# Two-layer attention stack and gated block on one core: the weighted sums for the gates and for layer 1's shift and scale, on GpSimd instead of VectorE

## The chip, the cores and the metric

The kernel runs on one NeuronCore of a Trainium2 chip. Its five engines have instruction queues of their own, each issued strictly in order: TensorE (PE in the profile; its weight loads are shown apart as PEld), VectorE (DVE), ScalarE (ACT), GpSimd (POOL) and SyncE (SP), which issues all of this kernel's DMAs. The metric is device time in microseconds, from one execution; lower is better. What can be told from no change in a measurement of this kernel is about 2%.

## The reference, cut to what matters

256 tokens of 1024 features pass through two layers with adaptive normalization, a final norm, and a second block (three gated branches and a feed-forward network). Everything is float32. What the change touches is `ada`, a product of one vector of 1024 features with a matrix:

```
c_act = jax.nn.silu(c)
for layer in range(DEPTH):
    ada = jnp.einsum('bd,de->be', c_act, w_ada[layer]) + b_ada[layer]
    shift, scale, gate = jnp.split(ada, 3, axis=-1)
    h = rms_norm(x, norm_g[layer]) * (1.0 + scale[:, None, :]) + shift[:, None, :]
    i = layer // 2
    if layer % 2 == 0:
        y = even_mixer(h, ...)
    else:
        y = odd_mixer(h, ...)
    x = x + gate[:, None, :] * y
return rms_norm(x, final_g)
```

## The kernel before, in words

Tokens lie in two tiles of 128, features in eight tiles of 128. A projection is a sum over feature tiles of matrix products of 128x128 by 128x512. For accuracy each float32 operand is split into a rounded part and the rest (`split`, line 616): ScalarE copies the rounded part into a tile of the pool `kr`, VectorE subtracts to get the rest into another, and TensorE makes three products of them (`mm3`). Weights come by DMA in pieces of 512 KB, 128x1024, into the pool `k4`, which has 13 slots and also holds other tiles of that size; a slot is free again once its piece has been split. So per piece VectorE and ScalarE work once, and TensorE 12 times.

The stages in the order of time: the norm of layer 0 and its first products (up to about 60 us); the rest of layer 0's projections with its attention between them, and the first half of its output projection (up to about 210 us); its second half, with the residual sum and the norm of layer 1 (`end0`, line 1372, and `next_tile`, line 1390); layer 1 (up to about 480 us); the second block.

`ada` is computed in two ways. Layer 0's shift and scale have code of their own (`ada_v`, `ada_p`), which the change leaves alone. For layer 0's gate and for all three parts of layer 1 there is `ada_row` (line 1284), called for eight chunks of 512 columns: two for `gate0`, two for the shift `B1`, two for the scale `A1`, two for layer 1's gate `gate1`. A chunk has eight feature tiles; the weights of two of them come in one DMA of 512 KB. `st["acc"]`, 128x512 from the pool `k2` (14 slots), is cleared by GpSimd, gets the bias in its first row by DMA, and is then added to eight times: weights times a column of `sc`, plus the sum so far, in one VectorE instruction. That makes 64 such instructions. Then `last` splits the sum (ScalarE, VectorE), TensorE multiplies both parts by ones (`onesr`), which adds up the 128 partitions and spreads the result over all of them, and the row is evicted from the PSUM bank `m`.

The order of the instructions is not written by hand. The program is run once as a draft, in which `Order` (line 127) collects every instruction with what it reads and writes; a list schedule with a price for each kind of instruction (`cost`, line 474) then sets the order on every engine and which slot each tile gets, and the program is issued in that order (`issue`, line 439). All instructions pass through one call, so the profile names line 527 for nearly all of them, and tiles are told by pool: `k` is `k4` or `k2`, `kr` the split parts, `acc` and `m` PSUM banks. Once the order is set, an engine that waits for an operand holds up all that is behind it in its queue; that holds for SP as well, where a load that waits for a slot holds up the loads behind it.

Of the kernel before, what the change touches and what calls it, by code (L numbers as in the profile page):

```python
# [21 lines left out]
P = 128  # L22
# [6 lines left out]
# columns of w_in_even, in the order in which the kernel uses them  # L29
# [9 lines left out]
def plan():  # L39
    """(name, where it comes from, k-tiles, columns, queue) of every weight chunk, in the order of use."""  # L40
# [65 lines left out]
# rows that are broadcast over the partitions  # L106
_ROWS = [("bg0", 1024), ("b1", 3072), ("g1", 1024), ("fg", 1024), ("mg", 1024), ("ffg", 1024),
         ("gb", 3072), ("sink", 8)]
# per-partition columns
# [17 lines left out]
class Order:  # L127
    """Collects the instructions of the kernel, with what each reads and writes, and issues them in the
    order of a list schedule: first by program order, then by the latest start that each instruction
    can have without lengthening the schedule found before. A tile takes any slot of its pool that is  # L130
    free by then, so long as every tile that still holds one can finish."""

    def __init__(self, nc, found):
        self.ops = []                  # [engine, call, duration, row share, tiles, predecessors, table, name, lag]
        self.hist = {}                 # tile -> [(region, op, writes)]
        self.tiles = {}                # tile -> its pool
        self.found, self.count = found, 0
        self.vector, self.scalar = Engine(self, "DVE", nc.vector), Engine(self, "ACT", nc.scalar)
        self.tensor, self.gpsimd = Engine(self, "PE", nc.tensor), Engine(self, "Pool", nc.gpsimd)
        self.sync = Engine(self, "SP", nc.sync)  # L140
        self.lag = 0.0

    def tile(self, pool, shape, dt):
        """a tile of the pool: a place of its own in the draft, a slot that is free by then in the issue"""
# [15 lines left out]
    def region(ap):  # L160
        """(partitions, elements) that an access covers, as bounds"""
# [44 lines left out]
    def gap(self, i, j):  # L206
        """from the end of op i to the start of op j that needs it"""
        a, b = self.ops[i], self.ops[j]
        return DELAY.get((a[0], b[0]), 230.0)
# [7 lines left out]
    def late(self, end):  # L217
        """the ops put as late as the engines allow, those first that ended last; the time from their start to the end"""
# [24 lines left out]
    def best(self, slack, rounds):  # L243
        self.links()
        # first the order of the program; then, from the order found, the ops as late as they may be
# [8 lines left out]
    def solve(self, slack, way):  # L254
# [5 lines left out]
        # tiles: the op that takes the slot, and the ops that hold it  # L260
# [20 lines left out]
        held = {}                                        # ops that wait for a slot, by pool  # L281
# [3 lines left out]
        def wants(i):  # L285
            """the tiles of op i that have no slot yet"""
            return [t for t in ops[i][4] if t not in slot]

        def safe(p, new):
            """whether the program's own order could still go on once `new` are taken as well"""  # L290
# [26 lines left out]
        def room(i):  # L317
            """when the slots that op i needs are there, or None"""
# [30 lines left out]
        while done < n:  # L349
# [36 lines left out]
            else:  # L386
                if e == "PE":
                    # the clock is halved after a tick with little to do
# [62 lines left out]
# from the end of an instruction to the start of one that needs it, by their engines  # L451
# [11 lines left out]
def columns(name, writes, reads):  # L463
    """what the clock's monitor counts of a matrix instruction: columns, by the share of the rows"""
# [9 lines left out]
def cost(engine, name, writes, reads, kw):  # L474
# [32 lines left out]
    if engine == "ACT":  # L507
        return (51.0 if psum else 93.0) + 0.833 * r + 93.0 * pointers, 230.0, SETS.get(kw.get("func"))
    return 80.0 + 0.75 * r, 230.0, None
# [22 lines left out]
def body(tc: tile.TileContext, *args, dbg=None):  # L532
    """The program runs twice: once to find the order of its instructions and the slots of its tiles,
    with nothing issued, and once to issue them."""
# [8 lines left out]
def program(ctx: ExitStack, tc: tile.TileContext, found, x_d, wst, rows, cols, rope, w2, out, dbg=None):  # L543
# [65 lines left out]
    def weight(key, part=0):  # L609
        """the two parts of a piece of the weights, loaded and split where it is first needed"""  # L610
# [17 lines left out]
    # ---------------- the tensor engine's order: products of the projections, and between every few  # L628
    # of them what else is due ----------------
# [29 lines left out]
    class Proj:  # L659
        """One chunk of 512 columns; lhs = (hi, lo), of four feature tiles [P, 4, 256] each; evict(tt, psum) per token tile."""  # L660
# [33 lines left out]
    def out_proj(tag, lhs, evict, mid):  # L694
        """two chunks; first the first half of the contraction, then the second, one token tile after the other"""
# [26 lines left out]
    # additive masks: token on the partition, key along the row  # L722
# [5 lines left out]
    # strictly causal, for both token tiles side by side, and a column past the end of each: there the scores are  # L728
    # large, so that a running product starts anew
# [10 lines left out]
    # compressed blocks: a token sees block n once it is at 16 n + 31 or past it  # L740
# [15 lines left out]
    def rsqrt(ssum, scale, n=1, post=None):  # L756
        """1 / sqrt(ssum * scale + EPS) of a [P, n] tile: a first guess from the bits, then Newton."""
# [7 lines left out]
        # r <- (v r r - 3 m) r leaves -2, 16 and -8192 times the root  # L765
# [19 lines left out]
    def to_lhs(lhs, src, tt, k0=0, nk=8, scale=None):  # L785
        """src [P tokens, nk*128] -> feature-major hi and lo."""
# [15 lines left out]
    def rope_to(outs, src, tt, n):  # L802
        """src [P, n*64] (PSUM) -> every AP of outs [P, n, 64]."""
# [10 lines left out]
    def silu_of(dst, z):  # L814
        """2 silu(z) = z (1 + tanh(z / 2)); z in PSUM."""
# [13 lines left out]
    def transposes(dst, src, n, p):  # L829
        """dst [P, n, 128] (SBUF) <- n transposed 128-column blocks of src, by way of the bank p."""  # L830
# [5 lines left out]
    # the heads of a unit lie on the same half of the partitions: products of different halves  # L836
    # run side by side and may not share a bank
# [3 lines left out]
    def sm_unit(tt, segs, klen, masks, o, den, sink=None):  # L841
        """segs: (pairs lhsT and rhs, values per key block, slot); masks: (view, rhs) adders on the scores.
        Three steps, each of which returns the next."""
# [59 lines left out]
    # =====================================================================================  # L903
    # layer 0
    # =====================================================================================
# [67 lines left out]
    kd = [t4([P, 5, 2, 64], n="kd") for _ in range(2)]        # ka, ks0, ks1, kw0, kw1, each twice  # L973
    kcr = t4([P, 2, 2, 2, 64], n="kcr")                        # [tt, (k, v), group, d]
    va = const.tile([P, 2, 64], F32, name="va")
    vsw = t4([P, 2, 2, 2, 64], n="vsw")                        # [tt, (slc, win), group, d]
    gb = const.tile([P, 2, 24], F32, name="gb")
    qaT = t2([P, 4, P], n="qaT")                               # the first token tile
    qaS, qbS = (t4([P, 2, 4, P], F32R) for _ in range(2))      # the second, in two parts (see `stack`)
    qbT = t4([P, 4, 256], n="qbT")  # L980
    kT = t2([P, P], n="kaT")
    kaS = t4([P, 2, 256], F32R)                                # [part, token]
# [881 lines left out]
```

## Time and profile before

| what | us |
|---|---|
| runs of the kernel | 807.18, 811.31, 822.17 (median 811.31) |
| span of the profiled execution | 810.1 |
| TensorE busy | 786.1 |
| VectorE busy | 601.2 |
| ScalarE busy | 393.8 |
| GpSimd busy | 8.8 |

The span is the time from the first to the last instruction of one profiled execution. Busy is the time in which at least one instruction of the engine runs; since products are pipelined, TensorE shows as busy when it is merely full of overlapping work. The granted clock (PEclk) is the share of 2.4 GHz that TensorE was given; it has two levels, 1.00 and 0.50 (1.2 GHz), and a stretch shows the mean. A line of a group has the mean duration of one instruction in ns; an idle time with a releaser is what the engine waited for just before.

### The profile page before, as it was taken

What the parts mean: (1) busy time and instruction counts of PE and PEld (TensorE: products, weight loads), DVE (VectorE), ACT (ScalarE), POOL (GpSimd) and SP (SyncE); (2) the same over time, 40 slices, a digit from 0 to 9 for tenths busy, and PEclk for the clock granted to TensorE, in tenths of its full rate; (3) what the DMA queues carried; (4) which work ended last, traced back from release to release, by engine and by line L of the source; (5) the groups of instructions that cost most, each with busy time, mean ns of one, the idle gap of its engine ahead of it and who ended that gap; (6) DMA issues with size and microseconds to landing.
All of it is one profiled execution on the core that took longest, in us unless ns stands there. A gap on an engine that the chain in (4) does not pass through costs nothing.

```text
span 810.1 us, 10521 instructions
## 1 busy us (share of the span) xinstructions
PE 786.1 (97%) x3716; PEld 617.3 (76%) x3716; DVE 601.2 (74%) x1129; ACT 393.8 (49%) x683; POOL 8.8 (1%) x34
## 2 busy tenths in 40 slices
PE   4999999999799999999999999999999999999998
PEld 3886567778677777777887777888887888888886
DVE  7989877868998644657879999999887555556541
ACT  4363556544355644554665545456465543445410
POOL 2000000000000000000000000000000000000000
PEclk9999999978899999999999999999999999999999
DMA  9995677445386325272753446654484645646301
GB/s 334 336 329 175 207 261 235 152 185 177 108 324 241 113 81 182 75 234 77 264 189 108 136 137 218 210 197 133 161 292 150 227 155 177 201 143 221 116 1 52
DMA packets 43443, 148.11 MB, mean 183 GB/s; under 512 B 5880, under 2 KB 7288, under 8 KB 43392
## 3 DMA queue, kind: packets, MB, share of 16 engines
q1 hardware_dynamic: 43392, 147.46, 53.6%
q8 instruction: 29, 0.48, 0.2%
q14 instruction: 22, 0.18, 0.1%
HBM read 146.39 MB, written 1.05 MB: 182 GB/s over the span
## 4 chain that ended last, share of the span: by engine, by line
PE 90%; DMA 3%; DVE 3%; ACT 2%; issue 1%; ACTq 0%; SPq 0%
PE acc L527 71%; PE m L527 19%; DMA k<-in_wst_dram 3%; DVE k L527 2%; ACT kr L527 1%; ACT k L527 1%; DVE kr L527 1%; DMA x<-in_x_dram 0%; DVE tiny L527 0%; DVE ab L527 0%; DVE sc L527 0%; DVE b L527 0%; DVE qkn L527 0%; ACTq L527 0%; SPq L527 0%
## 5 line engine op out<-in xcount | busy, mean ns | idle before, releaser
L527 PE MATMUL acc<-kr,kr 128*128 128x512 f32 x2520 | 662.3, 409 | 3.8 <-ACT kr L527 3.4
L527 PEld LDWEIGHTS acc<-kr,kr 128*128 128x128 f32 x2520 | 469.9, 190 | 111.9 <-ACT kr L527 5.8
L527 DVE TENSOR_TENSOR kr<-k,kr 128x1024 fp32r<-128x1024 f32 (+3 forms) x238 | 269.2, 1144 | 81.3 <-PE acc L527 65.9
L527 ACT ACTIVATE kr<-k 128x1024 fp32r<-128x1024 f32 (+3 forms) x238 | 234.3, 998 | 190.1 <-PE acc L527 126.3
L527 PE MATMUL m<-identf,k 128*128 128x128 f32 (+1 forms) x434 | 103.0, 283 | 13.3 <-DVE sc L527 8.7
L527 PEld LDWEIGHTS m<-k,k 128*128 128x128 f32 (+1 forms) x404 | 67.6, 197 | 23.2 <-issue 13.3
L527 ACT ACTIVATE k<-m 128x512 f32<-128x512 f32 (+5 forms) x96 | 45.3, 489 | 78.1 <-PE m L527 73.3
L527 PE MATMUL m<-k,k 128*128 128x64 f32 (+3 forms) x404 | 82.7, 302 | 0.4 <-DVE k L527 0.4
L527 PEld LDWEIGHTS m<-identf,k 128*128 128x128 f32 (+1 forms) x434 | 60.7, 149 | 26.5 <-issue 16.9
L527 DVE SCALAR_TENSOR_TENSOR k<-k,sc,k 128x512 f32<-128x512 f32 (+1 forms) x112 | 69.1, 629 | 0.3
L527 DVE SCALAR_TENSOR_TENSOR k<-k,col,k 128x256 f32<-128x256 f32 x128 | 54.3, 476 | 0.0
L527 DVE TENSOR_REDUCE tiny<-m 128x2 f32<-128x512 f32 (+1 forms) x30 | 20.7, 692 | 43.1 <-PE m L527 42.3
L527 ACT ACTIVATE kr<-m 128x512 fp32r<-128x512 f32 (+3 forms) x56 | 27.3, 498 | 39.2 <-PE m L527 34.9
L527 ACT ACTIVATE k<-m,tiny 128x128 f32<-128x128 f32 (+1 forms) x80 | 32.8, 421 | 26.9 <-DVE tiny L527 12.7
L527 DVE TENSOR_TENSOR kr<-m,kr 128x512 fp32r<-128x512 f32 (+3 forms) x52 | 28.3, 557 | 8.5 <-ACT kr L527 6.1
L527 PE MATMUL m<-kr,kr 128*128 128x408 f32 (+2 forms) x96 | 29.9, 377 | 0.0
L527 DVE TENSOR_TENSOR k<-k,k 128x512 f32<-128x512 f32 (+4 forms) x41 | 25.0, 615 | 1.1 <-PE m L527 0.9
L527 PEld LDWEIGHTS m<-kr,kr 128*128 128x128 f32 (+1 forms) x96 | 18.8, 201 | 7.3 <-issue 4.1
L527 DVE SCALAR_TENSOR_TENSOR k<-acc,rf,k 128x256 f32<-128x256 f32 x22 | 10.4, 481 | 13.3 <-ACT k L527 13.1
L527 DVE SCALAR_TENSOR_TENSOR k<-k,acc 128x512 f32<-128x512 f32 x20 | 13.6, 682 | 7.5 <-PE acc L527 4.5
L527 ACT ACTIVATE k<-acc,rf 128x256 f32<-128x256 f32 x22 | 10.2, 472 | 17.3 <-PE acc L527 17.0
L527 DVE TENSOR_TENSOR k<-acc,x 128x512 f32<-128x512 f32 x4 | 2.8, 692 | 20.4 <-PE acc L527 20.4
(100 smaller groups left out, 337.3 us busy)
## 6 DMA issues: line engine op xcount, KB each, us to landing
k<-in_wst_dram SPq DMA_DIRECT2D x266, 512.0 KB, 4.3
k<-in_rows_dram SPq DMA_DIRECT2D x4, 512.0 KB, 4.0
k<-in_wst_dram SPq DMA_DIRECT2D x8, 204.0 KB, 4.4
k<-in_rows_dram SPq DMA_DIRECT2D x6, 256.0 KB, 5.2
x<-in_x_dram SPq DMA_DIRECT2D x2, 512.0 KB
out_dram<-k SPq DMA_DIRECT2D x4, 256.0 KB, 2.0
k<-in_w_dram SPq DMA_DIRECT2D x2, 128.0 KB
rp<-in_rope_dram SPq DMA_DIRECT2D x1, 128.0 KB, 6.5
```

The lines of the kernel that those rows point to most:

```text
L527: self._o.add(self._n, lambda: f(*a, **kw), method, writes, reads, info)
```

## The change

In `ada_row` the one VectorE instruction becomes two on GpSimd: the weights are multiplied in place by the column of `sc`, and the product is added to the sum. The price list of the schedule gets an entry for a GpSimd addition. Comments are taken out elsewhere.

```diff
@@ cost
     if engine == "ACT":
         return (51.0 if psum else 93.0) + 0.833 * r + 93.0 * pointers, 230.0, SETS.get(kw.get("func"))
+    if name == "tensor_tensor":
+        return 100.0 + 2.2 * r, 230.0, None
     return 80.0 + 0.75 * r, 230.0, None
@@ ada_row, part
-                V.scalar_tensor_tensor(st["acc"], st["raw"][:, r % 2, :], sc[:, r:r + 1], st["acc"], op0=ALU.mult, op1=ALU.add)
+                w = st["raw"][:, r % 2, :]
+                G.tensor_scalar(w, w, sc[:, r:r + 1], None, op0=ALU.mult)
+                G.tensor_tensor(st["acc"], w, st["acc"], op=ALU.add)
                 if r == 7:
                     after(3, last)
```

The schedule is made anew, so the order of all engines and the slots differ. In the rows below, a name with two numbers is a tile: `k46_67` is slot 6 of `k4`, `k20_107` slot 0 of `k2`, `sc_179` the column of weights.

First VectorE and GpSimd where the first chunk of `gate0` is summed, just after layer 0's first products. Before, on VectorE:

```order
L527 SCALAR_TENSOR_TENSOR k20_107<-k46_67,sc_179,k20_107 128x512
L527 TENSOR_TENSOR k47_68<-k211_118,k29_116 128x128
L527 SCALAR_TENSOR_TENSOR k20_107<-k46_67,sc_179,k20_107 128x512
L527 TENSOR_TENSOR k211_118<-k210_117,k212_119 128x512
L527 TENSOR_TENSOR k47_68<-k25_112,k26_113 128x128
L527 TENSOR_TENSOR k210_117<-acc3_150,rp_172 128x512
L527 SCALAR_TENSOR_TENSOR k20_107<-k40_61,sc_179,k20_107 128x512
L527 TENSOR_TENSOR k212_119<-k28_115,k210_117 128x512
L527 TENSOR_TENSOR kr18_95<-m3_157,kr18_95 128x128
L527 SCALAR_TENSOR_TENSOR k20_107<-k40_61,sc_179,k20_107 128x512
L527 TENSOR_TENSOR kr18_95<-m2_156,kr18_95 128x128
```

Now on GpSimd, from its last early clear to the end of that chunk:

```order
L529 MEMSET k45_66 128x2x2
L529 TENSOR_SCALAR k412_73<-k412_73,sc_179 128x512 x2
L529 TENSOR_TENSOR k20_107<-k412_73,k20_107 128x512 x2
L529 TENSOR_SCALAR k46_67<-k46_67,sc_179 128x512 x2
L529 TENSOR_TENSOR k20_107<-k46_67,k20_107 128x512
L529 TENSOR_SCALAR k411_72<-k411_72,sc_179 128x512
L529 TENSOR_TENSOR k20_107<-k46_67,k20_107 128x512
L529 TENSOR_SCALAR k411_72<-k411_72,sc_179 128x512
L529 TENSOR_TENSOR k20_107<-k411_72,k20_107 128x512
L529 TENSOR_SCALAR k412_73<-k412_73,sc_179 128x512
L529 TENSOR_TENSOR k20_107<-k411_72,k20_107 128x512
L529 TENSOR_SCALAR k412_73<-k412_73,sc_179 128x512
```

The additions into `k20_107` are gone from VectorE and stand on GpSimd, each with a multiplication ahead of it.

Next TensorE at the border of layer 0 and layer 1, where the first half of the output projection ends (`acc3_150`), the finished rows are added up (`onesr`), and the transposes for the second half come (`identf`). Before:

```order
L527 MATMUL acc3_150<-kr11_88,kr1_78 128x512
L527 MATMUL m3_157<-kr16_93,onesr_174 128x512 x2
L527 MATMUL m1_155<-kr22_99,onesr_174 128x512
L527 MATMUL m2_156<-kr19_96,onesr_174 128x512
L527 MATMUL m1_155<-kr22_99,onesr_174 128x512
L527 MATMUL m2_156<-kr19_96,onesr_174 128x512
L527 MATMUL m0_154<-kr23_100,onesr_174 128x512 x2
L527 MATMUL m2_156<-identf_160,k412_73 128x128 x4
L527 MATMUL acc0_147<-kr18_95,kr15_92 128x512
L527 MATMUL acc0_147<-kr20_97,kr15_92 128x512
```

Now:

```order
L529 MATMUL acc3_150<-kr18_95,kr3_80 128x512
L529 MATMUL m0_154<-kr13_90,onesr_174 128x512 x2
L529 MATMUL m1_155<-kr25_102,onesr_174 128x512
L529 MATMUL m3_157<-kr16_93,onesr_174 128x512
L529 MATMUL m1_155<-kr25_102,onesr_174 128x512
L529 MATMUL m3_157<-kr16_93,onesr_174 128x512
L529 MATMUL m2_156<-kr15_92,onesr_174 128x512 x2
L529 MATMUL m1_155<-kr12_89,onesr_174 128x512
L529 MATMUL m2_156<-identf_160,k49_70 128x128 x4
```

Four rows were taken there, both parts of each; now it is these four and the first part of a fifth, `kr12_89`, the first chunk of `gate1`, whose second part stands about a hundred rows further down.

Last SP's queue, with what each load waits for, at about the second and third chunk. Before:

```order
L527 DMA k46_67<-in_wst_dram 128x1024 [waits DMAHW6_49,DVE_49]
L527 DMA k40_61<-in_wst_dram 128x1024 [waits DMAHW7_49,DVE_49]
L527 DMA k410_71<-in_wst_dram 128x1024 [waits DMAHW1_49,DVE_49]
L527 DMA k212_119<-in_rows_dram 1x512 [waits DMAHW0_49,Pool_49]
L527 DMA k412_73<-in_wst_dram 128x1024 [waits DMAHW3_49,DVE_49]
L527 DMA k27_114<-in_rows_dram 1x512 [waits DMAHW2_49,Pool_49]
L527 DMA k411_72<-in_wst_dram 128x1024 [waits PE_49]
L527 DMA k43_64<-in_wst_dram 128x1024 [waits DMAHW4_49,PE_49]
L527 DMA k49_70<-in_wst_dram 128x1024 [waits DMAHW5_49,PE_49]
L527 DMA k410_71<-in_wst_dram 128x1024 [waits DMAHW7_49,DMAHW6_49,DVE_49]
L527 DMA k46_67<-in_wst_dram 128x1024 [waits PE_49]
```

Now:

```order
L529 DMA k412_73<-in_wst_dram 128x1024 [waits DMAHW3_49,DMAHW1_49,Pool_49]
L529 DMA k49_70<-in_wst_dram 128x1024 [waits DMAHW2_49,PE_49,Activation_49]
L529 DMA k46_67<-in_wst_dram 128x1024 [waits DMAHW5_49,Pool_49]
L529 DMA k47_68<-in_wst_dram 128x1024 [waits DMAHW4_49,DVE_49]
L529 DMA k40_61<-in_wst_dram 128x1024 [waits PE_49,Activation_49]
L529 DMA k43_64<-in_wst_dram 128x1024 [waits DMAHW6_49,DMAHW0_49,DVE_49]
L529 DMA k411_72<-in_wst_dram 128x1024 [waits DMAHW7_49,Pool_49]
L529 DMA k412_73<-in_wst_dram 128x1024 [waits DMAHW1_49,Pool_49]
L529 DMA k213_120<-in_rows_dram 1x512 [waits Pool_49]
L529 DMA k47_68<-in_wst_dram 128x1024 [waits DMAHW4_49,DMAHW2_49,Pool_49]
L529 DMA k43_64<-in_wst_dram 128x1024 [waits DMAHW6_49,DMAHW3_49,Pool_49]
```

Loads of weights (`in_wst_dram`) that waited for VectorE to give a slot back wait for GpSimd now, where the slot held a piece of `ada`; the loads behind them in the queue include those for the projections.

## Rows read from the trace of the kernel before

**Rows 1.** The page, busy us (share of the span) and instructions of each engine.

```profile
PE 786.1 (97%) x3716; PEld 617.3 (76%) x3716; DVE 601.2 (74%) x1129; ACT 393.8 (49%) x683; POOL 8.8 (1%) x34
```

**Rows 2.** Windows by stage: length, busy us of each engine, PEclk, DMA share, GB/s.

```profile
0.00:60.00 60.00, 45.97 (x221) 38.85 (x222) 51.18 (x136) 28.61 (x49) 5.58 (x27) 1.00 0.93 334
60.00:110.00 50.00, 49.31 (x240) 30.05 (x239) 43.82 (x106) 23.90 (x66) 1.57 (x3) 1.00 0.60 201
110.00:164.00 54.00, 54.00 (x292) 40.29 (x290) 43.37 (x81) 30.85 (x94) 1.68 (x4) 1.00 0.63 217
164.00:200.00 36.00, 36.00 (x174) 29.86 (x173) 25.56 (x61) 17.73 (x35) 0.00 (x0) 0.76 0.47 165
200.00:222.00 22.00, 17.32 (x71) 13.69 (x70) 20.94 (x49) 8.18 (x16) 0.00 (x0) 0.84 0.37 117
222.00:262.00 40.00, 39.92 (x186) 31.20 (x184) 36.91 (x46) 21.06 (x25) 0.00 (x0) 1.00 0.78 283
262.00:480.00 218.00, 218.00 (x1049) 167.73 (x1047) 156.26 (x313) 115.07 (x202) 0.00 (x0) 1.00 0.43 142
480.00:810.00 330.00, 325.57 (x1496) 265.65 (x1496) 223.13 (x345) 148.43 (x200) 0.00 (x0) 1.00 0.51 168
```

**Rows 3.** The page, the chain that ended last, share of the span by engine.

```profile
PE 90%; DMA 3%; DVE 3%; ACT 2%; issue 1%; ACTq 0%; SPq 0%
```

**Rows 4.** The chain in order of time at the layer border: start, us, what.

```profile
212.23 1.70 ACT k L527 x4
213.94 2.71 issue
...
222.97 5.79 DMA k<-in_wst_dram
```

**Rows 5.** Timeline of DVE, first sum and layer border: start, us, form.

```profile
64.05 0.74 DVE L527 SCALAR_TENSOR_TENSOR k<-k,sc,k 128x512 f32<-128x512 f32 x1
...
205.10 0.74 DVE L527 SCALAR_TENSOR_TENSOR k<-k,sc,k 128x512 f32<-128x512 f32 x1
...
207.89 0.74 DVE L527 SCALAR_TENSOR_TENSOR k<-k,sc,k 128x512 f32<-128x512 f32 x1
```

**Rows 6.** DVE from 60 to 262 us by form: busy us, mean ns, idle before.

```profile
L527 DVE SCALAR_TENSOR_TENSOR k<-k,sc,k 128x512 f32<-128x512 f32 x64 | 47.0, 742 | 0.0
L527 DVE TENSOR_TENSOR kr<-k,kr 128x1024 fp32r<-128x1024 f32 x38 | 45.7, 1214 | 0.3 <-ACT kr L527 0.3
...
L527 DVE TENSOR_TENSOR k<-k,k 128x512 f32<-128x512 f32 x12 | 8.2, 683 | 0.9 <-PE m L527 0.9
...
L527 DVE TENSOR_TENSOR kr<-k,kr 128x512 fp32r<-128x512 f32 x8 | 5.4, 681 | 0.5 <-ACT kr L527 0.5
...
L527 DVE SCALAR_TENSOR_TENSOR k<-k,tiny,k 128x512 f32<-128x512 f32 x4 | 2.9, 744 | 0.0
...
L527 DVE TENSOR_TENSOR k<-x,k 128x512 f32<-128x512 f32 x4 | 2.7, 682 | 0.0
L527 DVE TENSOR_TENSOR x<-x,k 128x512 f32<-128x512 f32 x4 | 2.7, 688 | 0.0
```

**Rows 7.** All of POOL by form.

```profile
L527 POOL MEMSET k<- 128x512 f32 x10 | 5.2, 525 | 109.1 <-PE m L527 85.7 <-ACT kr L527 13.9 <-DVE kr L527 9.5
...
L527 POOL TENSOR_SCALAR_AFFINE_SELECT mc<-mc 128x16 f32<-128x16 f32 x2 | 0.3, 198 | 0.0
...
masks.py:199 POOL TENSOR_SCALAR_AFFINE_SELECT identf<-identf 128x128 f32<-128x128 f32 x1 | 0.3, 292 | 0.1
```

**Rows 8.** Timeline of PE at the layer border.

```profile
210.63 2.03 PE L527 MATMUL m<-kr,onesr 128*128 128x512 f32 x8
216.65 0.66 PE L527 MATMUL m<-identf,k 128*128 128x128 f32 x2 [3.99 <-issue]
```

**Rows 9.** Waits of SP's queue from 60 to 262 us: total, times, longest.

```profile
SPq L527 <- DVE k L527: 51.1, 20, 15.7
...
SPq L527 <- POOL k L527: 6.3, 2, 5.2
```

## The prediction

> **What bounds the kernel now.** I read the busy table first, then windows by stage, then the chain, then the forms of the two engines between which the work moves. The reader is to see in the busy table that TensorE is at 97% of the span and GpSimd at 1% [rows 1], and in the chain that 90% of it is TensorE's own work and 3% VectorE's [rows 3]. A VectorE at 74% is therefore no bound by itself. The windows say where it might still be one [rows 2]. From 110 to 164 us TensorE is busy for all 54 us, from 262 to 480 us for all 218. Idle it is 14.0 us up to 60 us, 0.7 us from 60 to 110, 4.7 us from 200 to 222 and 4.4 us after 480. The 64 sums all lie between 60 and 262 us [rows 6], so of TensorE's idle time only 0.7 + 4.7 + 0.1 = 5.5 us is there to be won.
>
> A second loss is the clock. It is 0.76 from 164 to 200 us and 0.84 from 200 to 222 us, at full speed elsewhere in this part [rows 2], which means stretches at 1.2 GHz; (1 - 0.76) x 36 + (1 - 0.84) x 22 = 12.2 us is what they cost at most. Before the first fall VectorE is far from full, 25.56 of 36 us; TensorE is in the short products of the attention there, full by its records.
>
> **What is removed.** 64 instructions of 742 ns, 47.0 us of VectorE, with no idle time before them [rows 6]. Behind a full TensorE this is worth nothing; it counts where TensorE waits for VectorE. That place is the layer border. TensorE adds up the finished rows from 210.63 us and then stands still for 3.99 us ahead of the transposes of layer 1's input [rows 8]; in the chain this is the norm of layer 1, on ScalarE and VectorE [rows 4], and VectorE is busy for 20.94 of the 22 us [rows 2]. But only two of the sums stand ahead of that norm there, at 205.10 and 207.89 us [rows 5]. So the gain on the path is 2 x 0.74 = 1.5 us. The other 62 I cost at nothing; the cover is TensorE's own queue, and if that cover were not full, the 5.5 us above would be their limit. The stall behind the border that ends with a load of weights of 5.79 us [rows 4] depends on slots and not on VectorE's load, and I leave it as it is.
>
> **What is added.** 64 multiplications and 64 additions on GpSimd, 128x512 each. The trace has no GpSimd instruction that reads two tensors. A clear of that size, which only writes, takes 525 ns. An operation with one input takes 198 ns for 16 elements and 292 ns for 128 [rows 7], which is 0.84 ns an element on a fixed 185 ns, and makes 292 + 384 x 0.84 = 615 ns for 512. Lower end of a step of one multiplication and one addition: two clears, 1.05 us. Upper end: every tensor read or written is a pass of its own, two for the multiplication and three for the addition, 5 x 0.43 + 2 x 0.185 = 2.52 us. I take 0.62 us, and for the addition a second read behind the first, 0.62 + 0.43 = 1.05 us, together 1.66 us, because the one-input operation is the nearest row. 64 steps are then 106 us (67 to 161). The Trainium skill, page "GPSIMD Engine Reference", section "Elementwise — side-by-side cycle accounting", has 4497 ns for an addition of 2048 elements; an estimate from it is 1.1 us for 512 and 1.7 us a step, 109 us in all.
>
> GpSimd has the time. Its only other work from 60 to 262 us is 3.3 us of clears [rows 2]. The tightest stretch is from the first sum, 64.05 us [rows 5], to the row at the border, 210.63 us [rows 8]: by then TensorE's new order wants the first part of a fifth row there, beside two earlier ones, so seven chunks or 56 steps must be done in 146.6 us, 2.6 us each. At 1.66 us that is 93 us, cover for 53 us of waiting.
>
> Three queues now wait for GpSimd. ScalarE's copy of a finished sum waits, and behind it are the copies of weights; TensorE's product with ones waits, and behind it everything; and SP's loads wait for the slots of `ada` pieces, with the projections' weights behind them. SP waited for such slots before as well, 51.1 us for VectorE's work on `k` tiles in 20 waits, without TensorE running dry [rows 9]; with a slot held for two steps of 1.66 us instead of two of 0.74 it is held 1.8 us longer, and I cost that at 0 as long as GpSimd keeps its pace. Its clears for attention and for new sums stand behind sums in the same queue; they are few and early.
>
> **What may be paid twice.** While GpSimd reads, VectorE may have to wait, or the other way round. No row shows the two at work together on tensors, so the cost is bounded from both sides. Below: 0. Above: they exclude each other whenever a VectorE instruction takes two inputs from SBUF. The large ones of that kind between 60 and 262 us are 45.7 + 8.2 + 5.4 + 2.9 + 2.7 + 2.7 = 67.6 us in 70 instructions [rows 6]. GpSimd holds the inputs for 106 of 198 us, 54% of the time; what is left of an operation when another arrives is (0.62² + 1.05²) / (2 x 1.67) = 0.44 us on average, so a wait is 0.24 us. From 204 to 222 us I count 27 such instructions, large and small, in VectorE's timeline; if all wait, the border grows by 27 x 0.24 = 6.5 us. I take the middle, 3.2 us, as no row is nearer to either end. Elsewhere VectorE has won 47 us and pays back less than that, so TensorE stays covered.
>
> On this the Trainium skill has a rule against the change: "SBUF — State Buffer", section "Who interferes with whom", says that a VectorE instruction with two SBUF inputs and a GpSimd instruction that reads SBUF lock each other out for a whole instruction. No run here shows it yet; by that rule the upper end holds, and its result is the first rival.
>
> **The sum.** 810.1 us of the profiled span - 1.5 + 3.2 = 811.8. The median of the runs is 811.3, 1.2 us above the span, which I add: 813. Within the forecast's own range of 806 to 820 lie the 0 and the 6.5 us above, and some us from a new order that moves the clock's stretches. The products are the same ones in much the same sequence, so I expect a stretch at 1.2 GHz at the end of the attention again.
>
> **Rivals.**
> 1. Reads exclude each other throughout, GpSimd keeps its pace: 810.1 - 1.5 + 6.5 + 1.2 = 816. For it speaks how much of VectorE's work has two inputs; against it nothing that a row could show. Within 2% all the same.
> 2. Slower: GpSimd falls behind. It has 2.6 us for a step. With the upper end of 2.52 us and two waits for VectorE (67.6 of 202 us, a third of the time, half of about 1 us left: 0.17 us each) a step is 2.9, and with the slots that then come back late to SP some 3.0 us: 56 x 3.0 = 168 us instead of 146.6, TensorE stands 21.5 us longer at the border, 833 us. For it: queues in order, SP's loads behind GpSimd, a fifth row wanted at the border. Against it: it needs 1.8 times the price that the nearest rows give. It decides from 2.6 us on; at 3.2 us it would be 844.
> 3. Faster: the relief lets the norm and the attention end sooner, and both the 4.7 us of idle time and the 12.2 us of clock go: 810.1 - 16.9 + 1.2 = 794. For it: VectorE is 95% busy from 200 to 222 us. Against it: only three of the sums are in that window, and the clock falls while VectorE is not full.
>
> That the change does not do what it says is out: the order has 128 more tensor instructions on GpSimd, and 64 fewer on VectorE.
>
> **How the numbers follow.** About 2%, 16 us, is what a measurement of this kernel can tell from no change: faster is below 795, slower above 827.5. Forecast 0.47, rival 1 0.15, rival 2 0.30, rival 3 0.08. The first two are within 2% (0.62), the third gives slower (0.30), the fourth faster (0.08). The range reaches from near rival 3 to near the far end of rival 2: 797 to 842.
>
> **What would show it.** Right: VectorE's busy time falls by 40 to 47 us, GpSimd's rises by about 106, TensorE's busy time and its idle time at the border stay within some us, and the clock is low again in the last part of the attention. Exclusion would show as two-input instructions of VectorE with a mean well above 1214 ns and 683 ns while those with one SBUF input keep theirs. Rival 2 would show as waits of ScalarE, TensorE and SP for GpSimd, and a GpSimd without idle time up to the border. Wrong I am if TensorE's idle time between 60 and 262 us grows by more than 16 us, or nearly vanishes along with the low clock.

## The result, and the profile after

The changed kernel takes 864.0 us (median of 4 runs, 861.33 to 868.46) against 810.6 us for the kernel before on the same chip. The ratio is 1.067 with a 95% interval of 1.0615 to 1.0726: slower, by 53 us, and outside the range of 797 to 842. Some runs of these kernels are slow, at a lower clock; one of the four of before is (822.17 us, without which the difference is 54 us), and ratios and the medians of the experiments are of the other runs. The profiled execution spans 859.6 us, 49.5 more than before.

The busy times of the changed kernel, on the page, stand against [rows 1]:

```profile
PE 805.5 (94%) x3716; PEld 624.9 (73%) x3716; DVE 587.0 (68%) x1065; ACT 393.7 (46%) x683; POOL 208.3 (24%) x162
```

GpSimd has taken on 199.5 us and not 106. VectorE has given up 47.0 us and yet fell by only 14.2: by the sum of durations it is 33 us longer in the work that it kept (22.8 us against the 564.2 us of cols8 below, which has the same order and hardly any work on GpSimd). TensorE has the same 3716 instructions; its idle time (span less busy time) went from 24.0 to 54.1 us, and its busy time up by 19.4 us. The two make the 49.5 us. The chain that ended last now has GpSimd in it, where [rows 3] had 90% of TensorE:

```profile
PE 70%; POOL 15%; DVE 7%; issue 3%; DMA 3%; ACT 1%; POOLq 0%; SPq 0%; DVEq 0%; ACTq 0%
```

The windows by stage, cut as in [rows 2] (length; busy us of PE, PEld, DVE, ACT, POOL; PEclk, DMA share, GB/s):

```profile
60.00:110.00 50.00, 46.23 (x195) 27.70 (x194) 32.38 (x76) 18.30 (x51) 44.81 (x34) 0.90 0.44 157
110.00:164.00 54.00, 50.21 (x254) 33.42 (x253) 33.08 (x57) 27.45 (x83) 45.11 (x30) 1.00 0.53 187
164.00:200.00 36.00, 27.73 (x120) 20.43 (x120) 11.70 (x20) 11.03 (x27) 36.00 (x25) 0.78 0.31 105
200.00:222.00 22.00, 18.28 (x82) 13.95 (x82) 14.11 (x27) 12.04 (x26) 21.84 (x16) 0.73 0.72 240
222.00:262.00 40.00, 30.73 (x125) 24.44 (x124) 34.59 (x64) 16.59 (x28) 29.13 (x20) 0.80 0.45 158
262.00:480.00 218.00, 211.46 (x1001) 164.15 (x1000) 141.78 (x266) 107.91 (x187) 21.82 (x12) 0.98 0.45 157
```

From 164 to 200 us GpSimd is busy for the whole 36 us, and TensorE, VectorE and ScalarE all have idle time at once. TensorE is idle for 28.8 us from 60 to 262 us (5.5 before), and the clock is at 0.73 to 0.80 for nearly 100 us, after windows in which TensorE had gaps. That the gaps brought it down is not shown: in the kernel before it fell to 0.76 behind 54 us without one [rows 2]. One minus the clock, times the length, adds up to 26.9 us from 60 to 262 us, where [rows 2] gave 12.2: stretches at 1.2 GHz are at most 14.7 of the 19.4 us of longer busy time.

GpSimd's two new forms:

```profile
L529 POOL TENSOR_SCALAR k<-k,sc 128x512 f32<-128x512 f32 x64 | 113.9, 1787 | 76.1 <-DMA k<-in_wst_dram 76.1
L529 POOL TENSOR_TENSOR k<-k,k 128x512 f32<-128x512 f32 x64 | 88.0, 1379 | 1.0
```

A step is 1.79 + 1.38 = 3.17 us, against the 1.66 us of the forecast. The 76.1 us of idle time include 49.7 us before the first step; from then to the border, 190 us, GpSimd rests for 15.8 us, 13.8 of them from 105 us on, for a load. Its timeline shows one multiplication with nothing in its way:

```profile
198.65 1.56 POOL L529 TENSOR_SCALAR k<-k,sc 128x512 f32<-128x512 f32 x1
```

Who waits for it (total, times, longest), from 56 to 290 us; in [rows 9] SP's queue waited 6.3 us for GpSimd:

```profile
ACT kr L529 <- POOL k L529: 39.5, 6, 9.6
...
PEld m L529 <- ACT k L529: 20.9, 17, 8.2
...
PE m L529 <- ACT k L529: 15.2, 7, 7.8
```

```profile
SPq L529 <- POOL k L529: 153.9, 33, 12.0
```

TensorE itself hardly waits for GpSimd: it waits for ScalarE, which stands in its own queue behind a copy that waits for GpSimd. The chain in order of time has GpSimd in long pieces up to 219 us, and again behind the border, where its last eight steps stand:

```profile
63.10 17.05 POOL k L529 x11
...
144.87 29.02 POOL k L529 x20
...
183.85 17.66 POOL k L529 x12
...
202.64 10.16 POOL k L529 x7
212.86 6.34 POOL k L529 x4
...
264.10 5.03 POOL k L529 x3
...
270.49 7.09 POOL k L529 x3
277.66 7.14 POOL k L529 x4
```

And the finished rows on TensorE, at 210.63 us in [rows 8], with the transposes of layer 1's input behind them:

```profile
246.19 2.03 PE L529 MATMUL m<-kr,onesr 128*128 128x512 f32 x8
249.38 0.50 PE L529 MATMUL m<-kr,onesr 128*128 128x512 f32 x1 [1.17 <-ACT k L529]
256.32 1.08 PE L529 MATMUL m<-identf,k 128*128 128x128 f32 x4 [6.44 <-DVE k L529]
```

So 246.19 - 210.63 = 35.6 of the 49.5 us are lost before the rows, and 13.9 behind them. Up to the rows TensorE has 19.8 us more idle time and is busy 15.8 us longer, in 969 instructions (968 before), at a mean clock of 0.91 (0.96 before). The rows follow on its own products without a gap, and it waits only 1.17 us among them: the time was lost on the way there. The longer idle time behind the rows, 6.44 us, ends with VectorE. Its forms from 60 to 290 us, against [rows 6]:

```profile
L529 DVE TENSOR_TENSOR kr<-k,kr 128x1024 fp32r<-128x1024 f32 x34 | 49.4, 1459 | 17.5 <-ACT kr L529 17.2
L529 DVE TENSOR_TENSOR k<-acc,rp 128x512 f32<-128x512 f32 x14 | 9.0, 681 | 0.0
...
L529 DVE TENSOR_TENSOR kr<-m,kr 128x512 fp32r<-128x512 f32 x10 | 6.8, 685 | 3.1 <-ACT kr L529 3.1
...
L529 DVE SCALAR_TENSOR_TENSOR k<-k,tiny,k 128x512 f32<-128x512 f32 x4 | 3.8, 960 | 0.0
L529 DVE TENSOR_TENSOR x<-x,k 128x512 f32<-128x512 f32 x4 | 3.7, 958 | 0.0
...
L529 DVE TENSOR_SCALAR tiny<-tiny 128x4 f32<-128x4 f32 x6 | 1.8, 298 | 0.1
```

and three of these forms in the kernel before, from 55 to 310 us:

```profile
L527 DVE TENSOR_TENSOR k<-acc,rp 128x512 f32<-128x512 f32 x24 | 15.5, 683 | 0.3 <-PE acc L527 0.3
...
L527 DVE TENSOR_TENSOR kr<-m,kr 128x512 fp32r<-128x512 f32 x10 | 6.9, 687 | 0.9 <-ACT kr L527 0.8
...
L527 DVE TENSOR_SCALAR tiny<-tiny 128x4 f32<-128x4 f32 x8 | 1.3, 162 | 0.1
```

With both inputs in SBUF these means rose: 1214 to 1459 ns, 744 to 960, 688 to 958. Not every such form did: `k<-x,k` of 128x512 took 686 ns, 682 before. With one input in PSUM (`acc`, `m`) they are 681 and 685, against 683 and 687. But VectorE's small TENSOR_SCALAR instructions, with one tensor input in SBUF, rose too, the last line from 162 to 298 ns. The profile alone thus offers two causes, GpSimd's own slowness and a lock between the two engines, and besides them a new order of all instructions, made with wrong prices. The experiments take these apart.

### The profile page after: what moved, and what is told of

It is laid out like the page before. It is cut to its first block, busy times and chain, and to the rows that moved or that the text cites. A ratio compares the mean times of both kernels' runs of the same rounds, so it can differ in the third digit from the quotient of the medians.

```text
span 859.6 us, 10605 instructions
## 1 busy us (share of the span) xinstructions
PE 805.5 (94%) x3716; PEld 624.9 (73%) x3716; DVE 587.0 (68%) x1065; ACT 393.7 (46%) x683; POOL 208.3 (24%) x162
## 3 DMA queue, kind: packets, MB, share of 16 engines
HBM read 146.39 MB, written 1.05 MB: 172 GB/s over the span
## 4 chain that ended last, share of the span: by engine, by line
PE 70%; POOL 15%; DVE 7%; issue 3%; DMA 3%; ACT 1%; POOLq 0%; SPq 0%; DVEq 0%; ACTq 0%
PE acc L529 59%; POOL k L529 15%; PE m L529 11%; DVE k L529 4%; DMA k<-in_wst_dram 3%; DVE kr L529 2%; DVE tiny L529 1%; ACT kr L529 0%; DVE x L529 0%; ACT k L529 0%; POOLq L1864 0%; SPq L529 0%; DVE ab L529 0%; POOLq L529 0%; DVEq L529 0%
## 5 line engine op out<-in xcount | busy, mean ns | idle before, releaser
L529 PE MATMUL acc<-kr,kr 128*128 128x512 f32 x2520 | 673.8, 413 | 3.0 <-ACT kr L529 2.9
L529 DVE TENSOR_TENSOR kr<-k,kr 128x1024 fp32r<-128x1024 f32 (+2 forms) x238 | 278.8, 1184 | 139.3 <-PE acc L529 72.6
L529 ACT ACTIVATE kr<-k 128x1024 fp32r<-128x1024 f32 (+2 forms) x238 | 234.0, 998 | 253.0 <-PE acc L529 130.2
L529 POOL TENSOR_SCALAR k<-k,sc 128x512 f32<-128x512 f32 x64 | 113.9, 1787 | 76.1 <-DMA k<-in_wst_dram 76.1
L529 PE MATMUL m<-k,k 128*128 128x64 f32 (+4 forms) x404 | 86.5, 309 | 6.1 <-ACT k L529 6.1
L529 POOL TENSOR_TENSOR k<-k,k 128x512 f32<-128x512 f32 x64 | 88.0, 1379 | 1.0
L529 PE MATMUL m<-kr,kr 128*128 128x408 f32 (+1 forms) x96 | 31.1, 383 | 8.0 <-ACT k L529 8.0
L529 PEld LDWEIGHTS m<-kr,kr 128*128 128x128 f32 x96 | 19.7, 206 | 18.1 <-ACT k L529 9.7
L529 DVE SCALAR_TENSOR_TENSOR k<-k,sc,k 128x256 f32<-128x256 f32 x48 | 22.4, 481 | 0.2
L529 ACT ACTIVATE k<-k 128x512 f32<-128x512 f32 (+4 forms) x28 | 15.4, 551 | 8.5 <-DVE k L529 8.2
```

Source lines behind the costliest of these rows:

```text
L529: self._o.add(self._n, lambda: f(*a, **kw), method, writes, reads, info)
```

## The experiments

Theories: 1, GpSimd's own 2.8 us a step make it late, and its lateness passes through the in-order queues of ScalarE, SP and TensorE; 2, VectorE and GpSimd lock each other out; 3, the schedule's wrong price; 4, the other order of the instructions costs by itself. In every kernel named "cols", the order of the instructions is that of its partner to the instruction.

**cols8** (the order alone)

```diff
-                G.tensor_scalar(w, w, sc[:, r:r + 1], None, op0=ALU.mult)
-                G.tensor_tensor(st["acc"], w, st["acc"], op=ALU.add)
+                a = st["acc"]
+                G.tensor_scalar(w[:, 0:8], w[:, 0:8], sc[:, r:r + 1], None, op0=ALU.mult)
+                G.tensor_tensor(a[:, 0:8], w[:, 0:8], a[:, 0:8], op=ALU.add)
```

(the prices in `cost` stay those of 512 columns)

> Leaves out 504 of the 512 columns of each of the 64 sums; every instruction of the changed kernel stands at its place in its order, only GpSimd's two are 128x8 instead of 128x512. Theory 1 (GpSimd's own 2.8 us a step sets the end): the time goes back to the kernel before, 803 to 820, with GpSimd's busy time under 60 us and a clock of 0.97 or more. Theory 2 (VectorE and GpSimd lock each other out): also back, since little is read; DVE's two-input 128x1024 back to about 1214 ns. Theory 4 (the new order alone costs): the time stays at 850 to 864.

Measured: 811.5 us, ratio 1.0014 (0.9978 to 1.005). Theory 4 falls: the new order, the 64 instructions that VectorE lost and the 128 that GpSimd got cost nothing together (a cost of one could hide a gain of another; a gain had little room: from 60 to 262 us TensorE had 5.5 us of idle time, and at most 12.2 us of low clock). Theories 1 and 2 both expected this. This run also shows the lock by itself, because GpSimd's instructions are so short. GpSimd's timeline (start, us):

```profile
122.16 1.06 POOL L531 TENSOR_SCALAR k<-k,sc 128x8 f32<-128x8 f32 x1 [1.56 <-DMA k<-in_wst_dram]
123.19 0.19 POOL L531 TENSOR_TENSOR k<-k,k 128x8 f32<-128x8 f32 x1
123.37 0.30 POOL L531 TENSOR_SCALAR k<-k,sc 128x8 f32<-128x8 f32 x1
123.64 0.20 POOL L531 TENSOR_TENSOR k<-k,k 128x8 f32<-128x8 f32 x1
```

and VectorE's over the same time:

```profile
121.82 1.23 DVE L531 TENSOR_TENSOR kr<-k,kr 128x1024 fp32r<-128x1024 f32 x1 [0.39 <-ACT kr L531]
```

The same multiplication takes 0.30 us alone and 1.06 us when VectorE's two-input instruction is under way: it ends 0.17 us after VectorE's. The Trainium skill, "SBUF — State Buffer", section "Who interferes with whom", calls the port pair that VectorE and GpSimd share an exclusive lock and says that issue order decides who blocks; this row agrees. The prices without a wait also follow: from 8 to 512 columns the multiplication goes from 0.30 to 1.56 us, 2.5 ns a column, and the addition from 0.20 to 1.26 us (a row of act_mult below), 2.1 ns. A step is 2.82 us without any wait.

**cols288** (as cols8, with 288 of the 512 columns)

> Leaves out 224 of the 512 columns of each of the 64 sums, in the changed kernel's own order; a step is then 0.56 of 2.82, about 1.6 to 1.8 us, the price that the prediction took (1.66). Theory 1: with that price the forecast holds, 806 to 825. Theory 2 (the excess goes with how long GpSimd reads and writes beside VectorE): about 811 + 0.56 x 53 = 841. Theory 4: 850 to 864.

Measured: 821.6 us, ratio 1.0134 (1.0093 to 1.0176).

```profile
L531 POOL TENSOR_SCALAR k<-k,sc 128x288 f32<-128x288 f32 x64 | 81.6, 1283 | 95.3 <-DMA k<-in_wst_dram 85.8 <-DVE k L531 9.5
L531 POOL TENSOR_TENSOR k<-k,k 128x288 f32<-128x288 f32 x64 | 58.6, 919 | 1.0
```

Theory 1's range held; a cost in proportion (841) is out. But the step came out at 2.20 us with the waits in it, and the time at 11 us over before. Even at about the price that the prediction took without waits, the move thus costs more than the 3.2 us given to the exclusion. How much of the 11 us is the lock this run does not say, since GpSimd has 4% of the chain here.

**memsets** (GpSimd's time without its data)

```diff
+                if method == "tensor_scalar":
+                    f1(*a, **kw)
+                for _ in range(2):
+                    self._r.memset(IDLE[-1], 1.0)
+                if method == "tensor_tensor":
+                    f1(*a, **kw)
```

(in `Engine`, for GpSimd's two instructions of cols8; `IDLE` holds a spare 128x512 tile)

> Leaves out 504 of 512 columns of each sum, in the changed kernel's own order, and gives GpSimd its time back as work on no data of VectorE: two fills of a spare 128x512 tile (525 ns each in the trace of before) with each of its two instructions, 2.6 us a step instead of 2.8 alone and 3.17 in the changed kernel. Theory 1 (GpSimd late, and who waits for it): 835 to 855, with POOL in the chain of waits. Theory 2 (the lock between VectorE and GpSimd): 811 to 822, and DVE's 128x1024 at about 1214 ns.

Measured: 849.1 us, ratio 1.046 (1.0404 to 1.0517). GpSimd's forms:

```profile
L532 POOL MEMSET idle<- 128x512 f32 x256 | 134.4, 525 | 9.8
L530 POOL TENSOR_SCALAR k<-k,sc 128x8 f32<-128x8 f32 x64 | 28.0, 438 | 78.1 <-DMA k<-in_wst_dram 78.1
L534 POOL TENSOR_TENSOR k<-k,k 128x8 f32<-128x8 f32 x64 | 20.6, 321 | 0.0
```

A step of 0.44 + 0.32 + 4 x 0.525 = 2.86 us, with hardly any data shared with VectorE, gives 37 of the 53 us. The chain that ended last has the same 15% of GpSimd:

```profile
PE 70%; POOL 15%; DMA 5%; DVE 5%; ACT 2%; issue 2%; SPq 0%; POOLq 0%; ACTq 0%; DVEq 0%
```

This is theory 1's range, not theory 2's. The fills kept their 525 ns beside VectorE, and VectorE's two-input 128x1024 form took 1221 ns. But one form of VectorE with one input did wait, here in memsets and then in cols8 (55 to 310 us):

```profile
L544 DVE TENSOR_SCALAR tiny<-tiny 128x8 f32<-128x8 f32 x6 | 2.6, 440 | 0.1
```

```profile
L531 DVE TENSOR_SCALAR tiny<-tiny 128x8 f32<-128x8 f32 x6 | 1.0, 167 | 0.1
```

One of them took 0.53 us from 100.36 us on, when nothing but three fills in a row (99.75 to 101.44 us) ran on GpSimd. So a GpSimd instruction that only writes can hold VectorE up as well. It was little here: VectorE's busy time is 566.8 us, against 564.2 in cols8. By size of the step (0.75, 2.20, 2.86 and 3.17 us) the four kernels in this one order take 811, 822, 849 and 864 us: 11 us for the first 1.45, then 42 us for the next 0.97. So from some point below 2.86 us on, a longer step costs several times more; four points do not place the bend, which the prediction had at 2.6 us.

**priced** and **priced_cols8** (the right price in the schedule)

```diff
     if name == "tensor_tensor":
-        return 100.0 + 2.2 * r, 230.0, None
-    return 80.0 + 0.75 * r, 230.0, None
+        return 100.0 + 2.5 * r, 230.0, None
+    if name == "tensor_scalar":
+        return 120.0 + 3.25 * r, 230.0, None
+    return 80.0 + 0.75 * r, 230.0, None
```

> The same work as the changed kernel, with the two durations of GpSimd in the schedule's costs set to what the trace of after shows (1.78 and 1.38 us), so that the order is made for them. Theory 3 (the wrong price in the schedule): 811 to 826. Theory 1: GpSimd still needs 56 steps x 2.82 = 158 us from 56 us on, to 214, where the first shift row was asked for at 210; the order can hide most of it, 815 to 845. Theory 2: VectorE's lost 33 us stay, 840 to 864.

> The order of priced to the instruction, with 504 of 512 columns of each sum left out. Theory 1 with the lock (GpSimd's own time and VectorE's waits for it make priced's 847): 808 to 820. Theory 4 (the order that was made around a slower GpSimd is a worse one): 830 to 847.

Measured: priced 844.1 us, ratio 1.0424 (1.0359 to 1.0488); priced_cols8 812.7 us, ratio 1.0025 (0.9983 to 1.0067). The price in the schedule is worth about 20 us; with it GpSimd is gone from the chain:

```profile
PE 78%; DVE 13%; DMA 3%; issue 3%; ACT 2%; SPq 0%; DVEq 0%; ACTq 0%
```

Yet 34 us stay. The 844.1 lies in the ranges of both theory 1 and theory 2, and priced_cols8 shows that the 34 us are not the order's. What remains has VectorE in the chain with 13%, against 4% in priced_cols8 and 3% before [rows 3], and SP waits only 2.7 us for GpSimd: VectorE's busy time is 615.7 us in priced and 566.5 in priced_cols8, with the same instructions.

**gate1_only** and **gate1_cols8** (16 sums, beside the layer border; priced as above)

```diff
+                if tag[:4] == "ada1" and int(tag[4:]) >= 4:
+                    G.tensor_scalar(w, w, sc[:, r:r + 1], None, op0=ALU.mult)
+                    G.tensor_tensor(st["acc"], w, st["acc"], op=ALU.add)
+                else:
+                    V.scalar_tensor_tensor(st["acc"], w, sc[:, r:r + 1], st["acc"], op0=ALU.mult, op1=ALU.add)
```

> Only the 16 sums of layer 1's gate, due last, stand on GpSimd (45 us there, at the right price); the other 48 stay on VectorE as before. Theory 1: nothing waits for them, 803 to 818. Theory 2: a quarter of the excess, about 811 + 13 = 824. Theory 4: above 830.

> The order of gate1_only to the instruction, with 504 of 512 columns of its 16 GpSimd sums left out. Theory 2 (there the 16 sums stand beside VectorE's work at the layer border, and lengthen it): back to 805 to 815. Theory 4 (that kernel's other order costs its 15 us): stays at 820 to 828.

Measured: gate1_only 825.4 us, ratio 1.0199 (1.0141 to 1.0257); gate1_cols8 812.0 us, ratio 1.0022 (0.9989 to 1.0056). Theory 1 alone fails here: hardly anything waits for these sums (ScalarE once, 1.4 us; SP 2.6 us from 150 to 310 us, 1.2 in the partner), and GpSimd has no share in the chain. The windows of the border, first gate1_only and then gate1_cols8:

```profile
200.00:262.00 62.00, 49.42 (x210) 37.51 (x210) 57.21 (x77) 27.86 (x39) 41.84 (x23) 0.92 0.55 195
```

```profile
200.00:262.00 62.00, 57.07 (x251) 44.40 (x249) 47.96 (x78) 28.66 (x40) 7.85 (x20) 0.94 0.60 218
```

VectorE is busy 9.3 us longer in 77 instructions than in 78, and TensorE idle 7.7 us longer, at the one place where TensorE waits for VectorE. That is the lock with next to nothing else beside it.

**gate1_late, gate1_behind and their controls** (the same 16 sums, held back)

```diff
+    V.scalar_tensor_tensor(sc2, x[:, 1, D - 8:D], 0.0, sc, op0=ALU.mult, op1=ALU.add)
...
-                    G.tensor_scalar(w, w, sc[:, r:r + 1], None, op0=ALU.mult)
+                    G.tensor_scalar(w, w, sc2[:, r:r + 1], None, op0=ALU.mult)
```

(gate1_behind takes `sc2` from the last piece of layer 1's transposed input instead of `x`; the controls use `sc2` in VectorE's one instruction.)

> The same 16 sums of layer 1's gate on GpSimd at full width, but held back until the residual of layer 0 is done (their scalar column is a copy that VectorE makes from it), so that they stand behind the border, from about 250 us on, where VectorE is busy 27 of 50 us and off the chain. Theory 2, as far as the lock costs only where VectorE is on the path: 803 to 813. If the lock cost anywhere: 820 to 828 as in gate1_only.

> The control to gate1_late: the same 16 sums held back in the same way, but left on VectorE as one instruction each. If the move behind the border alone gives or costs something, both show it; both 803 to 815, and within 4 us of each other if the lock costs nothing there.

> As gate1_late, but the scalar column now depends on the last piece of layer 1's transposed input, so the 16 GpSimd sums start behind the whole border (about 250 us) and not in its tail (gate1_late's began at 220 us). If the lock costs only where VectorE is on the path: 803 to 812, within 4 us of its control. If it costs wherever GpSimd and VectorE meet: 816 to 822 again.

> The control: the same 16 sums held back to the same point, on VectorE. 803 to 812, as gate1_late_dve (807.6).

Measured: gate1_late 818.9 us, ratio 1.0111 (1.0078 to 1.0144); its control 807.6 us, ratio 0.9953 (0.9927 to 0.998). gate1_late's sums still began at 220 us, in the tail of the border, and its expectation of 803 to 813 was missed. gate1_behind, from 232 us on and not from the 250 expected: 814.6 us, ratio 1.0045 (1.0012 to 1.0078), against 811.1 us, ratio 0.9991 (0.996 to 1.0022), for its control. The same 32 GpSimd instructions thus cost 13 us at the border (against gate1_cols8), 11 in its tail and 4 behind most of it. The two intervals of the last pair overlap a little, and its 814.6 lies between the two ranges expected; that the lock costs nothing where VectorE is off the path is therefore not shown, only that it costs much less.

gate1_late_dve, with none of the sums on GpSimd, is 0.5% below before, with an interval that ends below 1. That is far less than the 2% that can be told from no change, and its cause was not tried.

**act_mult** and **act_mult_cols8** (the multiplication on ScalarE, the addition on GpSimd)

```diff
-                G.tensor_scalar(w, w, sc[:, r:r + 1], None, op0=ALU.mult)
+                S.activation(w, w, AF.Copy, scale=sc[:, r:r + 1])
                 G.tensor_tensor(st["acc"], w, st["acc"], op=ALU.add)
```

> All 64 sums, with the multiply on ScalarE (about 0.6 us each, 39 us in all beside its 394) and only the add on GpSimd (1.26 us alone; its price in the schedule is set to that). Theory 1: a step then holds GpSimd some 1.4 to 1.7 us, below the 2.2 that already fitted in the run with 288 columns, so GpSimd leaves the chain: 811 to 825. Theory 2: the adds still meet VectorE, half of the lock's part of the 53 us stays: 815 to 830. Above 835: ScalarE's 39 us have come onto the path.

> The order of act_mult to the instruction: ScalarE's 64 multiplies at full width, the adds on 8 of 512 columns (504 left out). If the lock (GpSimd's 64 full adds beside VectorE) made act_mult's 22 us over before: 808 to 818. If ScalarE's 43 us on the path or the other order made them: 826 to 836.

Measured: act_mult 833.9 us, ratio 1.0276 (1.0223 to 1.033), above both theories' ranges though below ScalarE's 835; act_mult_cols8 812.8 us, ratio 1.0013 (0.9973 to 1.0054). So ScalarE's 43 us and the order cost nothing together, and the 21 us come from the 64 full-width additions, although GpSimd waits for ScalarE for 148 us in all. Its timeline at the border:

```profile
197.85 1.26 POOL L529 TENSOR_TENSOR k<-k,k 128x512 f32<-128x512 f32 x1 [3.79 <-ACT k L529]
207.65 13.39 POOL L529 TENSOR_TENSOR k<-k,k 128x512 f32<-128x512 f32 x7 [8.53 <-ACT k L529]
```

Seven additions in a row take 1.91 us each, beside 1.26 for one alone. VectorE's 128x1024 form from 55 to 310 us, in act_mult and in act_mult_cols8:

```profile
L529 DVE TENSOR_TENSOR kr<-k,kr 128x1024 fp32r<-128x1024 f32 x49 | 67.8, 1388 | 22.1 <-ACT kr L529 12.0 <-PE acc L529 8.4 <-ACT k L529 1.6
```

```profile
L529 DVE TENSOR_TENSOR kr<-k,kr 128x1024 fp32r<-128x1024 f32 x53 | 64.5, 1221 | 28.3 <-ACT kr L529 12.6 <-PE acc L529 10.9 <-issue 2.6
```

GpSimd has no share in act_mult's chain, but SP waits 49.1 us for it (27.8 in act_mult_cols8, both from 55 to 310 us). So the 21 us are not shown to be the lock's alone.

## Why the prediction was wrong

**What bounds the kernel, and what is removed.** Held. Freeing VectorE was worth next to nothing: cols8, where VectorE is busy 37.0 us less and GpSimd has almost nothing to do, is level with before. One reading was off: the chain at the border [rows 4] shows ScalarE and then "issue", not VectorE; only the changed kernel's trace names VectorE as what TensorE waits for there.

**The step that failed first: the price of a step, 1.66 us, with an upper end of 2.52.** It measured 2.82 us alone and 3.17 us in the kernel, beyond the upper end. Both terms were low. The multiplication, taken at 0.62 us from an operation with one input [rows 7], is 1.56 us alone: that row is a mask selection, another operation, and the nearness of its form said nothing about its pace. The addition, taken at 1.05 us, is 1.26 us; the Trainium skill's figure ("GPSIMD Engine Reference", section "Elementwise — side-by-side cycle accounting") gave an estimate of 1.1 us, and the measurement decides. The upper end was no bound, because it too was built from passes at the pace of that selection.

**"GpSimd has the time."** The point of decision was right and the side wrong. By the prediction seven chunks, 56 steps, had to be done before the rows at the border. The trace has the 56th sum end at 244.9 us and the rows begin at 246.19. From 56.0 to 246.2 us GpSimd is busy for 174.4 us, 3.1 us for each of the 56 steps. This is the mechanism of rival 2: GpSimd late, and the in-order queues of ScalarE, SP and TensorE behind it. Its place was another. It had TensorE stand 21.5 us longer at the border (33 us at 3.2 us a step). In the trace TensorE does not stand there for the sums; of the 35.6 us by which the rows came late, 19.8 are idle time spread over the way there and 15.8 are longer busy time, in part the lower clock, which neither the forecast nor the rival had. So it is partly luck that the 33 us come near the 35.6. Behind the rows came 13.9 us that the rival did not have either: 10.3 of idle time and 3.7 of busy time, with GpSimd's last eight steps in the chain.

**SP's slots at no cost.** This was on the condition that GpSimd keeps its pace, and so failed with it: 153.9 us of SP's waits are for GpSimd now. What these alone cost was not tried; they are part of memsets' 37 us.

**The exclusion, 0 to 6.5 us, taken at 3.2.** The mechanism is shown, the size was off. The wait for one instruction, 0.24 us, is near the rises of 0.22 to 0.27 us in the means above, but by luck: with the measured times (1.56 and 1.26 us, GpSimd busy for 174.4 of 190.2 us) the same formula gives 0.65 us. VectorE's two-input instructions met GpSimd less often, or later in its instructions, than the formula takes; which, no run shows. The border alone was put too low, 6.5 us at most: gate1_only, with a quarter of the sums beside it, cost 13 us more than its partner. And the cost elsewhere was left out, on the ground that VectorE had won 47 us there; act_mult cost 21 us more than its partner, though not all of it need be the lock. Rival 1 (816 us) had the same fault.

**The split of the 53 us.** The order, with VectorE's relief: none (cols8). GpSimd's time with nearly no lock: about 37 (memsets). The rest, some 15, is by subtraction the lock and what it adds to GpSimd's own step. The two do not simply add up: with the right price in the schedule GpSimd is off the chain and 34 us remain, with VectorE's share of the chain at 13%.

**What would show it.** Two of the prediction's own tests answered as it had said: idle time of TensorE from 60 to 262 us grew by 23 us, over the 16 that were to prove it wrong; and ScalarE, TensorE and SP waited behind GpSimd. The test for the exclusion did so in part: three two-input means rose and those with an input in PSUM did not, but TENSOR_SCALAR with one input in SBUF, which was to keep its mean, rose from 162 to 298 ns. The chances put 0.30 on this side, and the range ended at 842, near the 844 of a step of 3.2 us. The step was 3.17 us; what the range lacked was above all the 13.9 us behind the rows.

## What to carry to other kernels

An instruction that an engine has never run in the trace has no nearest row: the price of another operation on that engine is no price, and the bounds must be wide enough to pass the point at which the engine falls behind. Ask of a side engine whether it meets the due time of what hangs on it in every in-order queue, not whether it has idle time in all. And work on GpSimd that reads SBUF is not free for VectorE: here 16 sums cost 13 us beside the stretch where VectorE's two-input instructions are the path and 4 us behind it, so keep it away from such stretches, or leave it on VectorE.

## What was not expected of the hardware

GpSimd's multiplication of one 128x512 tensor by a column of scalars, 1.56 us, is slower than its addition of two tensors, 1.26 us. A GpSimd instruction on 8 columns can take as long as one on about 300 when VectorE is ahead of it: 1.06 us instead of 0.30. Fills of GpSimd ran at 525 ns (mean of 256), as in the kernel before, while VectorE worked beside them; VectorE's two-input instructions kept their pace beside the fills, but its small TENSOR_SCALAR instructions with one input did not, 440 ns instead of 167.
